# A fourth buffer for raw weights in the gate stage of a hybrid attention block, with evaluations one product later

## The chip, the cores and the metric

The kernel runs on one core of a Trainium2 chip. It is one launch: the weights and the input start in device memory (HBM) and the output ends there. The metric is the device time of the launch in microseconds (us). Five engines work beside each other, each in its own fixed order: PE (TensorE, matrix products), DVE (VectorE, elementwise), ACT (ScalarE, activation functions and copies), POOL (GpSimd) and SP (SyncE, which here only issues DMA transfers). They wait for each other through semaphores.

## The reference

Two layers of a transformer block on 512 tokens of width 1024, in float32. A layer is a feed-forward part, a token mix with three kinds of attention, and a second feed-forward part, with layer norms between. The change lies in the end of the token mix:

```python
o_a, o_b, o_c = _nsa(...), _swa_sink(...), _fox(...)            # each 512 x 512
g = jax.nn.sigmoid(h @ w_gate + b_gate).reshape(B, S, N_BRANCH, D)   # three gates, each 512 x 1024
merged = g[:, :, 0] * (o_a @ w_br_a) + g[:, :, 1] * (o_b @ w_br_b) + g[:, :, 2] * (o_c @ w_br_c)
return merged @ w_out
```

## The kernel before

All tiles have 128 partitions, and a float32 product is made of three products of a cheaper kind: each operand is split into a high part `hi` (a rounded copy, made by ACT) and a low part `lo` (what is left, by DVE), and PE computes hi·hi + hi·lo + lo·hi. So each block of weights goes through the same steps: SP issues the load of 512 KB into a buffer called `raw`; ACT writes `hi`; DVE writes `lo` and with that frees the `raw`; PE uses both. A branch's block is loaded by two transfers of 256 KB.

The `raw` buffers form a ring. In this stage it has three entries, all from the pool `wt`; `wraw()` takes the next one in turn, and the load into it waits on SP's queue until the DVE operation that read it last has ended. SP works through its loads strictly in order.

The gate stage computes for each of the three branches (`br` 0, 1, 2 for a, b, c) eight blocks `d` of 128 gate columns. The first few are computed by `plain` (24 products of 512 columns each, then a tanh on ACT, since the sigmoid is written by tanh). `branch` multiplies the attention output of a branch with two blocks of its weights, and DVE multiplies the result by the gate and adds it to `acc` (the `stt` and `tt` lines, called the evaluation here). From block (1, 6) on, `cycle` computes two gate blocks at a time by a Winograd scheme with 7 products for 8. An object `Two` holds the two raw blocks `rg` and `ru`; `sums` forms four sums of them on DVE (tile `ws`), and `hi("ug")`, `hi("u1")`, `hi("u2")`, `hi("ud")` split the four operands. A cycle's PE work is: `ga` (two products), `pa` (two), `pb` (one), two more into `ga`, then the branch products `brp` of the cycle. The two later products into `ga` overwrite what ACT copies out as `sn`, so PE waits there until that copy is done. Seven cycles follow each other: (1,6), (2,2), (2,4), (2,6), (0,2), (0,4), (0,6). The cycles (2,2) and (0,2) load two branch blocks, the others one; the second one's `hi` and `lo` go into the tile `wo`, and the attention output of the branch is split into `oh` and `ol` just before.

Through the whole stage PE, POOL, ACT and DVE run in the order in which the code is written (`in_order()`). SP's loads are ordered by the scheduler, from its own estimate of when a buffer comes free. `tick` lets POOL issue a transfer for a later stage (`ts`), paced by the tile named. PSUM tiles come from `ps()`, a ring of eight banks. The stage begins with `plain(2, 1)`, whose weights `gate_w(2, 1, wt)` are the first block loaded in it; before, that block is split while the last attention batch still runs. `gp` is the pool of this stage; its memory was the attention's before. `token_sums` makes the tile `mm` on which the Winograd products work, in steps (`some(2)`) between the first products.

Of the kernel before, what the change touches and what calls it, by code (L numbers as in the profile page):

```python
# [9 lines left out]
F32 = mybir.dt.float32  # L10
# [8 lines left out]
P = 128  # L19
S, D, F = 512, 1024, 2816  # L20
# [44 lines left out]
def body(tc, a, out, depth=DEPTH):  # L65
# [8 lines left out]
    wt = pool("wt")  # L74
# [6 lines left out]
    def ps(tag=None, name="ps", shape=(P, 512)):  # L81
        if tag is None:
            tag = PS_ALL[ring[0] % 8]
            ring[0] += 1
        return psp.tile(list(shape), F32, name=name, tag=tag, bufs=PS_TAGS[tag])
# [32 lines left out]
    def more_raws(p, n):  # L118
        raws.extendleft([(p, n)] * n)

    def less_raws(p):
        keep = [x for x in raws if x[0] is not p]
        raws.clear()
        raws.extend(keep)
# [6 lines left out]
    more = K()  # L131
# [44 lines left out]
    def mm3(o, w, k, vh, vl, first, last):  # L176
        hi, lo = w
        if lo is None:
            nc.tensor.matmul(o[0:64], hi[:, k, 0:64], vh, start=first, stop=False)
            nc.tensor.matmul(o[0:64], hi[:, k, 0:64], vl, start=False, stop=last)  # L180
            return
        nc.tensor.matmul(o, hi[:, k], vh, start=first, stop=False)  # L182
        nc.tensor.matmul(o, hi[:, k], vl, start=False, stop=False)  # L183
        nc.tensor.matmul(o, lo[:, k], vh, start=False, stop=last)  # L184
# [655 lines left out]
    def mix(l, wts, pend, done_ffn, xap, xa, nxt):  # L840
# [264 lines left out]
        class Swa:  # L1105
            br, nseg, ngrp = 1, 1, 1
# [53 lines left out]
        class Fox:  # L1160
            br, nseg, ngrp = 2, 2, 2
# [48 lines left out]
        class Nsa:  # L1210
            br, nseg = 0, 2
# [249 lines left out]
        def gate_ev(t, p, br, d):  # L1461
            nc.scalar.activation(t, p, AF.Tanh, scale=0.5, bias=bg[:, br, d:d + 1])
# [83 lines left out]
        gp = pool("gp", reuse_waits="tile")  # L1546
        acc = gp.tile([P, KD, S], F32, name="acc")
        ob = [gp.tile([P, 4, S], F32R, name=n) for n in ("oh", "ol")]
        gd = [gp.tile([P, 4, P], F32R, name=n) for n in ("dh", "dl")]
        g1 = [gp.tile([P, S], F32, name=f"g1{br}") for br in range(3)]  # L1550
        gw = a["w_gate"][l]
        tt, stt = nc.vector.tensor_tensor, nc.vector.scalar_tensor_tensor
        lo4, hi4, H1, H2 = slice(0, 4), slice(4, 8), slice(0, 256), slice(256, 512)
# [25 lines left out]
        def gate_w(br, d, pl):  # L1579
            r = raw_of(gw, br * D + d * P)  # L1580
            u = pair_of(pl)
            parts(*u, r)
            return u

        def branch_w(br, d, pl, now=True):
            r = wraw()
            v = wb[br].rearrange("(k p) f -> p k f", p=P)
            for j in range(2):
                nc.sync.dma_start(r[:, 4 * j:4 * j + 4], v[:, :, (d + j) * P:(d + j + 1) * P])
            if pl is op:  # L1590
                u = op.tile([P, 2, KD, P], F32R, name="wo", tag="o2")
                u = u[:, 0], u[:, 1]
            else:
                u = pair_of(pl)
            lo = high(*u, r)
            if not now:
                return u, lo
            lo()
            return u

        def tick(t):
            sums_step(t[:, 0:1] if len(t.shape) == 2 else t[:, 0, 0:1])
# [27 lines left out]
        class Two:  # L1630
# [14 lines left out]
            def hi(u, n):  # L1645
                x = {"ug": u.rg, "u1": u.x1, "u2": u.x2, "ud": u.ru[:, hi4]}[n] if n != "ug" else u.rg
                t = gd if n == "ud" else pair_of(more.pool if n == "ug" else wt)
                setattr(u, n, t)
                return high(*t, x)
# [11 lines left out]
        def gate_t(br, d):  # L1661
            g[br, d] = t = gp.tile([P, S], F32, name="t", tag="t", bufs=4)
            return t

        def plain(br, d, w, t=None):
            p = ps(name="gate")
            proj(p, w)
            t = gate_t(br, d) if t is None else t
            gate_ev(t, p, br, d)
            tick(t)  # L1670

        def branch(br, d, w, mid=None):
            for j in range(2):
                p = ps(name="brp")
                for k in range(4):
                    mm3(p, w, 4 * j + k, ob[0][:, k], ob[1][:, k], k == 0, k == 3)
                if mid and j == 0:
                    mid()
                t, o = g[br, d + j], acc[:, d + j]
                if br == 1:  # L1680
                    stt(o, t, 1.0, p, op0=OP.add, op1=OP.mult)
                else:
                    stt(t, t, 1.0, p, op0=OP.add, op1=OP.mult)
                    tt(o, o, t, op=OP.add)
            tick(o)

        def temp(n):
            return gp.tile([P, S], F32, name=n, tag=n, bufs=2)

        def cycle(cur, nxt, brps, end):  # L1690
            ga, pa, pb = (ps(name="gate") for _ in range(3))
            none = lambda: None
            hi = nxt.hi if nxt else lambda n: none
            if nxt:
                nxt.sums()
            ws = [branch_w(br, d, op if i else wt, False) for i, (br, d) in enumerate(brps)]
            lo = hi("ug")
            prod(ga[:, H1], cur.ug, 0, XP)
            prod(ga[:, H2], cur.u1, 0, T[0], False)
            sn, v, h = temp("sn"), temp("v"), gate_t(cur.br, cur.d + 1)  # L1700
            nc.scalar.activation(sn, ga, AF.Copy)
            for _, f in ws:
                f()
            lo()
            prod(pa[:, H1], cur.u1, 4, T[1])
            lo = hi("u1")
            prod(pa[:, H2], cur.u2, 0, T[2], False)
            tt(v[:, H1], pa[:, H1], sn[:, H1], op=OP.add)
            tt(v[:, H2], pa[:, H2], v[:, H1], op=OP.add)
            tt(h[:, H2], sn[:, H2], v[:, H2], op=OP.add)  # L1710
            lo()
            prod(pb[:, H1], cur.ud, 0, T[3])
            lo = hi("ud")
            tt(h[:, H1], pb[:, H1], v[:, H2], op=OP.add)
            prod(ga[:, H1], cur.ug, 4, XR, False)
            lo()
            nc.scalar.activation(h, h, AF.Tanh, scale=0.5, bias=bg[:, cur.br, cur.d + 1:cur.d + 2])
            prod(ga[:, H2], cur.u2, 4, XS, False)
            t = gate_t(cur.br, cur.d)
            lo = hi("u2") if nxt else end()  # L1720
            tt(ga[:, H2], ga[:, H2], v[:, H1], op=OP.add)
            gate_ev(t, ga, cur.br, cur.d)
            lo()
            tick(t)
            for (br, d), (w, _) in zip(brps, ws):
                branch(br, d, w)

        wp = [gate_w(2, 1, wt)]
        split_o(1)
# [4 lines left out]
        def some(n):  # L1734
            for _ in range(n):
                steps.pop(0)()

        plain(2, 1, wp[0], g1[2])
        wp.append(gate_w(1, 3, wt))
        some(2)  # L1740
        branch(1, 0, wp[1])
        wp.append(branch_w(1, 2, more.pool))
        plain(1, 2, wp[2])
        some(2)
        wp.append(gate_w(1, 4, wt))
        plain(1, 3, wp[3])
        some(2)
        wp.append(gate_w(1, 5, wt))
        branch(1, 2, wp[4])
        some(2)  # L1750
        wp.append(branch_w(1, 4, more.pool))
        cur = Two(1, 6)
        plain(1, 4, wp[5])
        some(2)
        plain(1, 5, wp[6])
        some(2)
        some(2)
        cur.sums()
        los = [cur.hi(n) for n in ("ug", "u1", "u2", "ud")]
        for f in los:  # L1760
            f()
        branch(1, 4, wp[7])
        todo = deque([(2, 2), (2, 4), (2, 6), (0, 2), (0, 4), (0, 6)])
        then = Two(*todo.popleft())
        brps = {(1, 6): [(1, 6)], (2, 2): [(2, 0), (2, 2)], (0, 2): [(0, 0), (0, 2)]}

        wo, ws_ = a["w_out"][l], []
# [1 line left out]
        def out_w(k):  # L1769
            r = wraw()  # L1770
            nc.sync.dma_start(r.rearrange("p k f -> p (k f)"), wo[k * P:(k + 1) * P, :])
            u = pair_of(wt if k else more.pool)
            ws_.append(u)
            return high(*u, r)
# [5 lines left out]
        while cur:  # L1780
            me = cur.br, cur.d
            if me[1] == 2:
                split_o(me[0])
            if not then:
                out_w(0)()
            cycle(cur, then, brps.get(me, [me]), merged)
            cur, then = then, Two(*todo.popleft()) if todo else None
        los = [out_w(k) for k in (1, 2)]
        for d in (6, 7):
            los.append(high(mh[:, d], ml[:, d], acc[:, d]))  # L1790
        for f in los:
            f()
        more.n = 3
        order.__exit__(None, None, None)
        gp.release()
# [22 lines left out]
    w = xl[:, KD - 1, 256:512].bitcast(BF)  # L1818
    nc.vector.memset(w, 1.0)
    o = ps("po", "warm")  # L1820
# [155 lines left out]
```

## Time and profile before

| What | us |
|---|---|
| Median of 3 runs (lowest, highest) | 2467.86 (2467.81, 2469.29) |
| Profiled execution: its own time | 2468.07 |
| Profiled execution: span from first to last instruction | 2466.4 |
| PE busy in the span | 2423.0 (98%) |
| DVE, ACT, POOL busy | 1949.1 (79%), 1228.2 (50%), 487.4 (20%) |
| Gate stage of the first layer, about | 666 to 840 |
| Gate stage of the second layer, about | 1892 to 2078 |

PE's share of the chain that ended last is 96%, so time is saved here where PE waits or runs slowly, and nowhere else. A row of the timeline gives the start, the duration, the engine and line, what is written and read, and in brackets how long the engine was idle before it and what released it. A row of windows gives the busy time of PE, PEld (weight loads of PE), DVE, ACT and POOL in a stretch, with their counts, then PEclk, the share of its full clock that TensorE was granted, then the DMA share and the rate.

### The profile page before, as it was taken

The page shows a single profiled execution, that of the slowest core. Times are in us where ns is not written, and L with a number is a line of the kernel's source. Part 1 is how long each engine was busy: PE and PEld are TensorE (multiplying, and loading weights), DVE is VectorE, ACT ScalarE, POOL GpSimd, SP SyncE. Part 2 cuts the span into 40 slices and gives each one's busy share as a digit, 9 for nine tenths or more (in the row PEclk, how much of TensorE's full clock was granted, in tenths as well). Part 3 has the DMA queues.
Part 4 walks back from the last instruction along what each step waited for, and adds up shares of the span by engine and source line. Part 5 has one row for each costly group of instructions (what it writes and reads, how often), then busy time and mean ns, then how long its engine had stood idle before and what let it go on. Part 6 is the DMA issues. An engine that isn't in the chain of part 4 may idle for free.

```text
span 2466.4 us, 41973 instructions
## 1 busy us (share of the span) xinstructions
PE 2423.0 (98%) x15952; PEld 2168.5 (88%) x15952; DVE 1949.1 (79%) x3782; ACT 1228.2 (50%) x2336; POOL 487.4 (20%) x684
## 2 busy tenths in 40 slices
PE   9999999999998999999999999999999889999998
PEld 8999887888888889998899998878888788899987
DVE  6899976677677659999879998666775776699997
ACT  4444645676633434445534456356775333344463
POOL 4232402244310001124000003022453000000040
PEclk9999999999999999999999999999999999999999
DMA  7888754676563536787533346456665535333373
GB/s 204 231 223 218 255 166 124 173 164 142 120 167 89 170 121 154 207 212 238 185 106 108 104 148 224 143 146 183 151 142 135 148 90 171 103 94 103 104 240 123
DMA packets 422586, 390.09 MB, mean 158 GB/s; under 512 B 20472, under 2 KB 352392, under 8 KB 422384
## 3 DMA queue, kind: packets, MB, share of 16 engines
q1 hardware_dynamic: 385792, 287.00, 39.1%
q0 software_dynamic: 36592, 100.41, 16.9%
q8 instruction: 126, 2.06, 0.3%
q14 instruction: 76, 0.62, 0.1%
HBM read 360.02 MB, written 93.38 MB: 184 GB/s over the span
## 4 chain that ended last, share of the span: by engine, by line
PE 96%; DVE 2%; DMA 1%; ACT 1%; issue 1%; POOL 0%; SPq 0%; DVEq 0%; POOLq 0%; ACTq 0%
PE acc L331 17%; PE pg L647 17%; PE pu L647 8%; PE pj L182 6%; PE pj L183 6%; PE pj L184 5%; PE gate L1656 5%; PE pv L647 4%; PE brp L184 2%; PE brp L182 2%; PE brp L183 2%; PE sN L1258 2%; PE ptN L1300 1%; PE po L1319 1%; PE acc L196 1%; PE acc L197 1%
## 5 line engine op out<-in xcount | busy, mean ns | idle before, releaser
L162 DVE TENSOR_TENSOR lo<-raw,hi 128x1024 fp32r<-128x1024 f32 (+2 forms) x186 | 217.2, 1186 | 88.9 <-ACT hi L161 87.9
L182 PE MATMUL pj<-xh,hi 128*128 128x512 f32 (+1 forms) x720 | 267.7, 372 | 0.6 <-ACT hi L161 0.6
L184 PE MATMUL pj<-xh,lo 128*128 128x512 f32 (+1 forms) x720 | 255.0, 354 | 0.4 <-DVE lo L162 0.4
L183 PE MATMUL pj<-xl,hi 128*128 128x512 f32 (+1 forms) x720 | 254.9, 354 | 0.0
L161 ACT ACTIVATE hi<-raw 128x1024 fp32r<-128x1024 f32 (+2 forms) x186 | 185.8, 1019 | 131.3 <-PE acc L331 52.9
L647 PE MATMUL pg<-xl,hi 128*128 128x256 f32 x864 | 244.5, 283 | 0.0
L647 PE MATMUL pg<-xh,lo 128*128 128x256 f32 x864 | 244.5, 283 | 0.0
L647 PE MATMUL pg<-xh,hi 128*128 128x256 f32 x864 | 244.5, 283 | 0.0
L331 PE MATMUL acc<-hi,sh 128*128 128x512 f32 x568 | 221.5, 390 | 0.0
L331 PE MATMUL acc<-lo,sh 128*128 128x512 f32 x568 | 221.0, 389 | 0.0
L331 PE MATMUL acc<-hi,sl 128*128 128x512 f32 x568 | 221.0, 389 | 0.0
L352 POOL COPY pace<-sh 64x1 f32<-64x1 f32 x16 | 94.6, 5915 | 474.6 <-ACT sh L592 474.6
L544 DVE TENSOR_TENSOR lo<-ws,hi 128x1024 fp32r<-128x1024 f32 x144 | 175.0, 1216 | 0.0
L647 PEld LDWEIGHTS pg<-xh,hi 128*128 128x128 f32 x864 | 165.9, 192 | 0.2
L647 PEld LDWEIGHTS pg<-xl,hi 128*128 128x128 f32 x864 | 165.9, 192 | 0.2
L647 PEld LDWEIGHTS pg<-xh,lo 128*128 128x128 f32 x864 | 165.9, 192 | 0.0
L647 PE MATMUL pu<-th,hi 128*128 128x256 f32 x576 | 163.0, 283 | 0.0
L647 PE MATMUL pu<-tl,hi 128*128 128x256 f32 x576 | 163.0, 283 | 0.0
L647 PE MATMUL pu<-th,lo 128*128 128x256 f32 x576 | 163.0, 283 | 0.0
L184 PEld LDWEIGHTS pj<-xh,lo 128*128 128x128 f32 x720 | 136.4, 189 | 20.3 <-DVE lo L162 0.6
L541 ACT ACTIVATE hi<-ws 128x1024 fp32r<-128x1024 f32 x144 | 144.1, 1048 | 16.9 <-DVE ws L526 15.3
L182 PEld LDWEIGHTS pj<-xh,hi 128*128 128x128 f32 x720 | 136.8, 190 | 16.4 <-issue 3.7
(418 smaller groups left out, 7094.3 us busy)
## 6 DMA issues: line engine op xcount, KB each, us to landing
raw<-in_ffn_w_dram SPq DMA_DIRECT2D x228, 512.0 KB, 4.5
ts<-in_ffn_w_dram POOLq DMA_DIRECT2D x72, 768.0 KB, 7.2
raw<-in_w_in_dram SPq DMA_DIRECT2D x56, 512.0 KB, 4.1
raw<-ts SPq DMA_DIRECT2D x52, 512.0 KB, 4.1
raw<-in_w_gate_dram SPq DMA_DIRECT2D x48, 512.0 KB, 4.1
ts<-ts POOLq DMA_DIRECT2D x24, 768.0 KB, 8.4
x_sp<-xa POOLq DMA_DIRECT2D x24, 512.0 KB, 6.2
ks<-hl SPq DMA_DIRECT2D x96, 128.0 KB, 2.6
```

What stands on the lines that cost most here:

```text
L161: nc.scalar.activation(hi[:, c], raw[:, c], AF.Copy)
L162: nc.vector.tensor_tensor(lo[:, c], raw[:, c], hi[:, c].bitcast(F32), op=OP.subtract)
L182: nc.tensor.matmul(o, hi[:, k], vh, start=first, stop=False)
L183: nc.tensor.matmul(o, hi[:, k], vl, start=False, stop=False)
L184: nc.tensor.matmul(o, lo[:, k], vh, start=False, stop=last)
L331: nc.tensor.matmul(o, xx[:, t], ww[:, c], start=first and i == 0, stop=last and i == 2)
L352: nc.gpsimd.tensor_copy(pace[0:64], sp(min(p + 1, NS - 1))[0][0:64, 0, 0:1].bitcast(F32))
L541: nc.scalar.activation(t[0], x, AF.Copy)
L544: nc.vector.tensor_tensor(t[1], x, t[0].bitcast(F32), op=OP.subtract)
L647: nc.tensor.matmul(o, wx, vx, start=first and k == 0 and i == 0, stop=k == 3 and i == 2, skip_group_check=True)
L1258: nc.tensor.matmul(o[:, 0:nb].rearrange("p k b j -> p (k b j)"), q, kx[:, 2 * b0:2 * (b0 + nb)].rearrange("p a b -> p (a b)"), start=i == ...
L1656: nc.tensor.matmul(o, wx, vx, start=first and k == 0 and i == 0, stop=k == 3 and i == 2, skip_group_check=True)
```

## The change

- The ring of `raw` buffers gets a fourth entry, in the pool `gp` (`more_raws(gp, 1)`), taken first; to make room `sn` and `v` have one buffer each instead of two.
- `plain` and `branch` return their evaluation instead of doing it; in the first part of the stage each is placed after the next product, so on ACT and DVE it comes behind the splits and sums for that next product.
- In `cycle` the raw blocks of the cycle after the next are requested before the branch products, the four sums of the next cycle stand on DVE before the evaluations of the branch products, and the last evaluation of a cycle goes into the next one, behind the copy `sn`.

PE and POOL keep their order. The core of the diff:

```diff
+        more_raws(gp, 1)
...
         def plain(br, d, w, t=None):
             p = ps(name="gate")
             proj(p, w)
-            t = gate_t(br, d) if t is None else t
-            gate_ev(t, p, br, d)
-            tick(t)
+            def ev():
+                o = gate_t(br, d) if t is None else t
+                gate_ev(o, p, br, d)
+                tick(o)
+            return [ev]
...
         def temp(n):
-            return gp.tile([P, S], F32, name=n, tag=n, bufs=2)
+            return gp.tile([P, S], F32, name=n, tag=n)
...
-        def cycle(cur, nxt, brps, end):
+        pend_ev = []
+        def cycle(cur, nxt, brps, load, end):
...
-            if nxt:
-                nxt.sums()
             ws = [branch_w(br, d, op if i else wt, False) for i, (br, d) in enumerate(brps)]
-            lo = hi("ug")
+            los = [f for _, f in ws] + [hi("ug")]
...
             nc.scalar.activation(sn, ga, AF.Copy)
-            for _, f in ws:
+            for f in pend_ev + los:
                 f()
-            lo()
+            pend_ev.clear()
...
-            for (br, d), (w, _) in zip(brps, ws):
-                branch(br, d, w)
+            new = load()
+            for i, ((br, d), (w, _)) in enumerate(zip(brps, ws)):
+                evs = [branch(br, d, w, j) for j in range(2)]
+                if new and not i:
+                    new.sums()
+                if i == len(brps) - 1:
+                    pend_ev.append(evs.pop())
+                for f in evs:
+                    f()
+            return new
...
-        plain(2, 1, wp[0], g1[2])
-        wp.append(gate_w(1, 3, wt))
         some(2)
-        branch(1, 0, wp[1])
...
+        evs = plain(2, 1, wp[0], g1[2])
+        for i, (go, prep) in enumerate((
+                (lambda: [branch(1, 0, wp[1], j) for j in range(2)], lambda: gate_w(1, 3, wt)),
+                (lambda: plain(1, 2, wp[2]), lambda: branch_w(1, 2, more.pool)),
...
+            w = prep()
+            some(2)
+            new = go()
+            for f in evs:
+                f()
+            evs = new
...
         los = [out_w(k) for k in (1, 2)]
+        pend_ev.pop()()
...
+        less_raws(gp)
```

Three places show what this does to the order. Numbers at the names tell tiles apart; a tile can have another number in the changed kernel. First, ACT at the start of the stage in the first layer, before (`raw_7773` is the block for `plain(2, 1)`, `raw_7783` the one for `branch(1, 0)`, `pj` are the last gate products of the attention stage):

```order
L1532 ACTIVATE o2_4103<-po_7721 128x128
L1532 ACTIVATE o0_4101<-po_7721 128x128
L1462 ACTIVATE g10_7766<-pj_7518,bgate_82 128x512
L1462 ACTIVATE g11_7767<-pj_7631,bgate_82 128x512
L1559 ACTIVATE oh_7762<-o1_4102 128x1024 x2
L1559 ACTIVATE hi_7786<-raw_7783 128x1024
```

And the same place after the change:

```order
L1532 ACTIVATE o2_4103<-po_7721 128x128
L1532 ACTIVATE o0_4101<-po_7721 128x128
L1462 ACTIVATE g10_7766<-pj_7518,bgate_82 128x512
L1462 ACTIVATE g11_7767<-pj_7631,bgate_82 128x512
L1560 ACTIVATE hi_7775<-raw_7773 128x1024
L1560 ACTIVATE oh_7762<-o1_4102 128x1024 x2
L1560 ACTIVATE hi_7786<-raw_7783 128x1024
```

The split of the first block, which stood earlier, among the work of the last attention batch, now stands behind the last attention output `o0`. Next, SP's loads around the cycles (1,6) and (2,2), before (`raw_8123` is the branch block of (1,6), `raw_8268` and `raw_8270` the gate blocks of (2,4), `raw_8284` and `raw_8290` the two branch blocks of (2,2)):

```order
L1589 DMA raw_8123<-in_w_br_b_dram 128x4x128 x2
L1576 DMA raw_8268<-in_w_gate_dram 128x8x128
L1576 DMA raw_8270<-in_w_gate_dram 128x8x128
L1589 DMA raw_8284<-in_w_br_c_dram 128x4x128 x2
L1589 DMA raw_8290<-in_w_br_c_dram 128x4x128 x2
L1576 DMA raw_8467<-in_w_gate_dram 128x8x128
```

And after (`raw_8121`, `raw_8240`, `raw_8242`, `raw_8283` and `raw_8289` are the same blocks; `raw_8407` belongs to (2,6)):

```order
L1590 DMA raw_8121<-in_w_br_b_dram 128x4x128 x2
L1577 DMA raw_8240<-in_w_gate_dram 128x8x128
L1590 DMA raw_8289<-in_w_br_c_dram 128x4x128 x2
L1577 DMA raw_8242<-in_w_gate_dram 128x8x128
L1590 DMA raw_8283<-in_w_br_c_dram 128x4x128 x2
L1577 DMA raw_8407<-in_w_gate_dram 128x8x128
```

Before, `raw_8290` reuses the buffer of `raw_8284`, the load just ahead of it. After, the second branch block stands first of the two; it takes the buffer of `raw_8121`, and `raw_8283` takes that of the block split as `dh` in the cycle (1,6). Last, DVE around the end of the cycle (2,2), before (`lo_8402` is the last split of that cycle, `brp_…` its branch products, `ws_8474` the sums for (2,6)):

```order
L1560 TENSOR_TENSOR lo_8402<-ws_8279,hi_8401 128x1024
L1683 SCALAR_TENSOR_TENSOR g02_4277<-g02_4277,brp_8407 128x512
L1684 TENSOR_TENSOR acc_7761<-acc_7761,g02_4277 128x512
...
L1684 TENSOR_TENSOR acc_7761<-acc_7761,t_8324 128x512
L1640 TENSOR_TENSOR ws_8474<-raw_8469 128x512
L1641 TENSOR_TENSOR ws_8474<-ws_8474,raw_8467 128x512
L1642 TENSOR_TENSOR ws_8474<-raw_8467,raw_8469 128x512
L1643 TENSOR_TENSOR ws_8474<-raw_8467,ws_8474 128x512
```

And after, where the same sums are `ws_8437`:

```order
L1561 TENSOR_TENSOR lo_8402<-ws_8270,hi_8401 128x1024
L1641 TENSOR_TENSOR ws_8437<-raw_8409 128x512
L1642 TENSOR_TENSOR ws_8437<-ws_8437,raw_8407 128x512
L1643 TENSOR_TENSOR ws_8437<-raw_8407,raw_8409 128x512
L1644 TENSOR_TENSOR ws_8437<-raw_8407,ws_8437 128x512
L1687 SCALAR_TENSOR_TENSOR g02_4277<-g02_4277,brp_8411 128x512
L1688 TENSOR_TENSOR acc_7761<-acc_7761,g02_4277 128x512
```

The four sums moved from behind the eight evaluation rows to ahead of them.

More of the change, by code (lines that the diff above doesn't have):

```diff
@@ L1667, in plain, with branch, ev @@
             proj(p, w)
-            t = gate_t(br, d) if t is None else t
-            gate_ev(t, p, br, d)
-            tick(t)
[L1672 to L1678, printed above, removed]
+            def ev():
[3 more added lines that the diff above has]
+            return [ev]
+        def branch(br, d, w, j):
+            p = ps(name="brp")
+            for k in range(4):
+                mm3(p, w, 4 * j + k, ob[0][:, k], ob[1][:, k], k == 0, k == 3)
+            def ev():
                 t, o = g[br, d + j], acc[:, d + j]
@@ L1684, in branch @@
                     tt(o, o, t, op=OP.add)
-            tick(o)
+                if j:
+                    tick(o)
+            return ev
         def temp(n):
-            return gp.tile([P, S], F32, name=n, tag=n, bufs=2)
-        def cycle(cur, nxt, brps, end):
+            return gp.tile([P, S], F32, name=n, tag=n)
+        pend_ev = []
+        def cycle(cur, nxt, brps, load, end):
             ga, pa, pb = (ps(name="gate") for _ in range(3))
@@ L1736, in some, with load @@
                 steps.pop(0)()
-        plain(2, 1, wp[0], g1[2])
-        wp.append(gate_w(1, 3, wt))
         some(2)
-        branch(1, 0, wp[1])
[L1742 to L1757, printed above, removed]
+        todo = deque([(1, 6), (2, 2), (2, 4), (2, 6), (0, 2), (0, 4), (0, 6)])
+        def load():
+            return Two(*todo.popleft()) if todo else None
+        evs = plain(2, 1, wp[0], g1[2])
+        for i, (go, prep) in enumerate((
+                (lambda: [branch(1, 0, wp[1], j) for j in range(2)], lambda: gate_w(1, 3, wt)),
+                (lambda: plain(1, 2, wp[2]), lambda: branch_w(1, 2, more.pool)),
+                (lambda: plain(1, 3, wp[3]), lambda: gate_w(1, 4, wt)),
+                (lambda: [branch(1, 2, wp[4], j) for j in range(2)], lambda: gate_w(1, 5, wt)),
+                (lambda: plain(1, 4, wp[5]), lambda: branch_w(1, 4, more.pool)),
+                (lambda: plain(1, 5, wp[6]), load))):
+            w = prep()
[4 more added lines that the diff above has]
+            evs = new
+            if i < 5:
+                wp.append(w)
+        cur = w
+        then = load()
         cur.sums()
         los = [cur.hi(n) for n in ("ug", "u1", "u2", "ud")]
-        for f in los:
-            f()
-        branch(1, 4, wp[7])
-        todo = deque([(2, 2), (2, 4), (2, 6), (0, 2), (0, 4), (0, 6)])
-        then = Two(*todo.popleft())
+        new = [branch(1, 4, wp[7], j) for j in range(2)]
+        for f in los + evs:
+            f()
+        then.sums()
+        pend_ev.extend(new)
         brps = {(1, 6): [(1, 6)], (2, 2): [(2, 0), (2, 2)], (0, 2): [(0, 0), (0, 2)]}
@@ L1785, in mix @@
                 out_w(0)()
-            cycle(cur, then, brps.get(me, [me]), merged)
-            cur, then = then, Two(*todo.popleft()) if todo else None
+            new = cycle(cur, then, brps.get(me, [me]), load, merged)
+            cur, then = then, new
         los = [out_w(k) for k in (1, 2)]
+        pend_ev.pop()()
         for d in (6, 7):
```

## The prediction

> **What bounds the kernel now.** I read the page first (engines, then the chain that ended last), then PE's waits, then the clock.
>
> ```profile
> PE 2423.0 (98%) x15952; PEld 2168.5 (88%) x15952; DVE 1949.1 (79%) x3782; ACT 1228.2 (50%) x2336; POOL 487.4 (20%) x684
> PE 96%; DVE 2%; DMA 1%; ACT 1%; issue 1%; POOL 0%; SPq 0%; DVEq 0%; POOLq 0%; ACTq 0%
> ```
>
> PE bounds the kernel. The change gives PE the same products in the same order, so it can only move PE's idle time and its clock. The waits of PE over the whole span begin with:
>
> ```profile
> PE gate L1656 <- ACT sn L1701: 25.1, 6, 6.6
> PE gate L1656 <- DVE lo L1560: 4.3, 2, 2.1
> PE hid L1030 <- DMA cw<-in_cmp_k_w_dram: 1.9, 2, 1.3
> ```
>
> Columns: total us, times, longest. Both lie in the cycles (L1656 is `prod`), and the third wait is already small, so nearly all of PE's waiting is in the stage that the change touches: 29.4 us, in four places per layer. The windows behind the three larger places of each layer show a second cost (the seventh number after the length and the comma is the granted clock, 0.66 in the first row):
>
> ```profile
> 713.10:718.10 5.00, 4.96 (x29) 4.96 (x30) 4.97 (x7) 0.53 (x2) 0.00 (x0) 0.66 0.53 157
> 743.80:748.80 5.00, 5.00 (x26) 4.96 (x27) 4.26 (x8) 2.35 (x4) 0.00 (x0) 0.61 0.72 210
> 804.60:809.60 5.00, 5.00 (x25) 5.00 (x26) 4.12 (x7) 2.10 (x3) 0.00 (x0) 0.54 0.72 207
> 1938.50:1943.50 5.00, 5.00 (x29) 5.00 (x30) 4.97 (x7) 0.46 (x1) 0.00 (x0) 0.66 0.55 164
> 1969.10:1974.10 5.00, 4.98 (x26) 4.94 (x27) 4.24 (x8) 2.34 (x4) 0.00 (x0) 0.60 0.68 201
> 2029.60:2034.60 5.00, 4.97 (x23) 4.97 (x24) 4.20 (x7) 2.17 (x3) 0.00 (x0) 0.51 0.72 204
> ```
>
> After each such stall PE works for about four us at half clock. Lost in each: 5 us times one minus the clock, 1.70, 1.95, 2.30, 1.70, 2.00 and 2.45, together 12.1 us. The stalls therefore cost 29.4 + 12.1 = 41.5 us, and that is the most that the change can give.
>
> **The change part by part.** *The fourth buffer and the earlier loads.* The two long stalls of a layer are in the cycles with two branch blocks. PE, ACT and the chain at the first of them:
>
> ```profile
> 743.78 0.58 PE L1656 MATMUL gate<-xh,hi 128*128 128x256 f32 x1 [5.78 <-ACT sn L1701]
> 741.24 1.06 ACT L1559 ACTIVATE wo<-raw 128x1024 fp32r<-128x1024 f32 x1 [8.38 <-DMA raw<-in_w_br_c_dram]
> 736.34 1.14 DVE lo L1560
> 737.50 0.37 SPq L1589
> 737.92 3.25 DMA raw<-in_w_br_c_dram
> 743.24 0.49 ACT sn L1701
> ```
>
> The load of the second branch block waits for the split of the first (DVE `lo`, ending 737.5), because it has that block's buffer; ACT stands at it, and `sn`, two rows behind on ACT, is what PE needs. After the change it takes the buffer of the branch block of (1,6), free some 15 us earlier, and the first branch block takes the one that `dl` frees. That row, the ACT row at which it is then needed, and the landing times in this stage (last number, median us):
>
> ```profile
> 725.83 0.68 DVE L1560 TENSOR_TENSOR dl<-raw,dh 128x512 fp32r<-128x512 f32 x1
> 731.81 1.05 ACT L1559 ACTIVATE hi<-raw 128x1024 fp32r<-128x1024 f32 x1
> raw<-in_w_gate_dram SPq DMA_DIRECT2D x16, 512.0 KB, 5.7
> raw<-in_w_br_a_dram SPq DMA_DIRECT2D x8, 256.0 KB, 4.4
> ```
>
> Issue at 726.5, the second half 0.5 later, 4.4 to land: 731.4, 0.4 before ACT wants it. ACT then does `hi`, `wo` and `hi` of the next gate block (at 1.05 each, 734.6 at most) and `sn` (0.49), done by about 735.1. The last product of `pb` starts at 737.72:
>
> ```profile
> 737.72 0.28 PE L1656 MATMUL gate<-mm,dl 128*128 128x256 f32 x1
> ```
>
> So PE does not wait, with 2.5 us in hand for a late load. The same holds at (0,2) with the loads of branch a. The small wait of (1,6) has ACT at a branch load, too, which now follows an earlier split:
>
> ```profile
> 722.21 0.38 PE L1656 MATMUL gate<-xh,hi 128*128 128x256 f32 x1 [0.37 <-ACT sn L1701]
> 719.67 2.01 ACT L1559 ACTIVATE hi<-raw 128x1024 fp32r<-128x1024 f32 x2 [6.04 <-DMA raw<-in_w_br_b_dram]
> ```
>
> I take all 25.1 us as gone. The transfers are the same in number and size.
>
> *Evaluations one product later.* The `lo` stall (2.14 us) ends the chain tanh, `mm`, `x`, sums, `lo`:
>
> ```profile
> 705.37 0.69 ACT L1462 ACTIVATE t<-gate,bgate 128x512 f32<-128x512 f32 x1 [4.23 <-PE gate L184]
> 713.14 0.38 PE L1656 MATMUL gate<-xh,lo 128*128 128x256 f32 x1 [2.14 <-DVE lo L1560]
> ```
>
> ACT waits 4.23 us for PE at a tanh that, after the change, comes behind the four splits of the first cycle. Everything behind it moves up by as much, more than the 2.14 needed: 4.3 us gone. The evaluations that wait instead have no reader before the next branch product or cycle, and PSUM has eight banks; for the two evaluations of a branch that means two banks held one product longer. Cost nothing, hidden by PE's own next product.
>
> *The first block of the stage.* It now goes into the buffer in `gp`, and its split stands behind the attention's last output. Rows of ACT and PE at that place, of the split before the change (ACT, DVE), and of DVE's last attention work:
>
> ```profile
> 667.03 1.27 ACT L1462 ACTIVATE g<-pj,bgate 128x512 f32<-128x512 f32 x2
> 668.17 2.03 ACT L1559 ACTIVATE oh<-o 128x1024 fp32r<-128x1024 f32 x2
> 665.94 0.72 PE L1319 MATMUL po<-p,v 128*64 128x128 f32 x10
> 667.15 0.40 PE L184 MATMUL gate<-xh,lo 128*128 128x512 f32 x1
> 643.52 1.05 ACT L1559 ACTIVATE hi<-raw 128x1024 fp32r<-128x1024 f32 x1
> 644.74 1.23 DVE L1560 TENSOR_TENSOR lo<-raw,hi 128x1024 fp32r<-128x1024 f32 x1
> 650.47 0.42 DVE L1098 CUSTOM_DVE_ANT_0 p<-sN,tab 128x256 f32<-128x256 f32 x1
> 661.23 0.69 DVE L885 COPY p<-ptN 128x512 f32<-128x512 f32 x1 [1.23 <-PE ptN L1300]
> ```
>
> ACT starts `hi` where `oh` started, 668.17, ends at 669.22; `lo` takes 1.23 more: 670.5. The third matmul of the stage, which ran at 667.15, needs that `lo`: PE loses 3.35 us per layer, 6.7 in all. This is a new stall, and it costs the clock too; the nearest row is the 2.14 us stall with 1.70, so 3.4 for two. The load waits for a DVE operation of the attention (in the built order the one of the 650.47 row); even behind DVE's last one, 661.92 + 5.7 = 667.6 is in time. Behind PE's last attention product, 666.66, it would be 672.4 and `lo` at 674.7: 7.5 us per layer. That is the upper end, 3.35 the value, zero the lower end, if ACT got to the split earlier.
>
> *The sums ahead of the evaluations* put 4 × 0.65 = 2.6 us of DVE work ahead of `ol` in the two cycles that split a new attention output, and `wo` must wait for `ol`. That eats up to 0.6 of the 2.5 us in hand; PE pays nothing. One buffer for `sn` and `v`: both are read within the cycle, no cost.
>
> *The attention's last batch.* ACT and DVE lose one split (1.05, 1.23) and a few rows there change places, one PSUM copy coming some 1.4 us later:
>
> ```profile
> 640.00:666.00 26.00, 26.00 (x208) 21.86 (x206) 13.81 (x48) 12.46 (x42) 12.36 (x21) 1.00 0.45 81
> ```
>
> PE is busy 26.00 of 26.00 us there and ACT under half, so I take zero; nothing can be gained, and 1.4 per layer may be lost.
>
> *Sum.* Gone: 29.4 + 12.1 = 41.5. New: 6.7 + 3.4 = 10.1. Net 31.4 us. The profiled execution took 2468.07, so 2436.7; the median of the runs is 0.2 lower, so **2436.5**.
>
> **The rivals.** *(A) The start stall costs no clock.* The gap is split in two (2.6 us, two matmuls, 0.8 us), and a clock that looks at longer stretches might not fall. Against it: the 2.14 us stall fell to 0.66 in both layers. Time 2436.5 − 3.4 = 2433.1. The Trainium skill says this in "TensorE: Matmul & The Clock Gate", Part 1: the clock halves after an idle window of about 3.4 us. By that rule the 2.14 us stall should have kept its clock; this trace disagrees.
>
> *(B) The first block lands late*, by the 7.5 us case above: 15.0 of stall, clock 2 × 2.45 = 4.9, so new costs of 19.9 for 10.1: 2446.3.
>
> *(C) Part of the double-branch stalls stays*, because branch loads land over 2.5 us later than the median, queued behind gate blocks. One us of stall in each of four places and 2.0 of clock: 12 more, 2448.5.
>
> *(D) No change that can be seen.* ACT is freed of the load and the same wait returns at `wo` behind `ol`, so that the two long stalls stay at three quarters: 0.75 × (24.4 + 8.7) = 24.8 given back (24.4 is 25.1 less the two small waits of (1,6), 8.7 the clock behind those four), 2461; with (B) besides, 2471. Little speaks for it, as `ol` ends 0.6 later where 2.5 are free.
>
> *(E) Slower: DVE stands at the sums.* They now wait for a gate block's load ahead of the evaluations and of the next cycle's `lo`. In the cycle (2,2) the load goes out when the `lo` in the first row below ends, and the sums come after the second:
>
> ```profile
> 743.47 1.22 DVE L1560 TENSOR_TENSOR lo<-raw,hi 128x1024 fp32r<-128x1024 f32 x1
> 749.66 1.23 DVE L1560 TENSOR_TENSOR lo<-ws,hi 128x1024 fp32r<-128x1024 f32 x1 [0.54 <-ACT hi L1559]
> PE brp L184: 33.6, 32
> ```
>
> That is 6.2 us against a landing of 5.7, hardly any reserve. But DVE can lose time: its idle time before the evaluations (the third row: total us, times) was 33.6 us for 14 cycles with their preludes, some 2.4 a cycle. With landings of x, PE would lose (x − 6.2 − 2.4) + 1.95 of clock in each of 12 cycles, and the gain of 31.4 is used up at x = 9.3 us. At 10.5 it is 12 × 3.85 = 46 us: 2483. Needed is a landing nearly twice the median.
>
> **How the numbers follow.** Forecast 0.63, A 0.12, B 0.08, C 0.10, D 0.03, E 0.04. The range of 8 in 10 or more runs from A with a little less stall at the start, 2431, to C, 2449; it takes in the 2.8 us of the attention and B. A change of 0.2% (5 us) is about what a measurement of this kernel can tell from none. Faster by more than that: the forecast, A, B, C, 0.93; within: 0.03; slower: 0.04.
>
> **What would show it.** In the profile after, `sn` and `lo` go from PE's waits in the cycles, and a new wait of PE at the first `gate` products (by `plain`, L182 and L184) of about 2.6 and 0.8 us per layer comes first in the list, with a granted clock near 0.66 in the five us behind it. ACT's waits for branch loads (8.4 us at `wo` in (2,2)) are gone. I am wrong if PE still waits for `sn` in (2,2) and (0,2), if the first wait is near 7 us, or if DVE idles over 2 us a cycle at the sums.

## The result and the profile after

| | before | after |
|---|---|---|
| Median of the runs, side by side (us) | 2468.57 (2467.81 to 2470.53) | 2433.74 (2432.91 to 2434.51) |
| Span of the profiled execution | 2466.4 | 2431.9 |
| PE busy | 2423.0 | 2412.5 |
| PE idle (span less busy) | 43.4 | 19.4 |
| Mean granted clock | 0.991 | 0.997 |

The change makes the kernel faster: after to before is 0.9858, with an interval of 0.9841 to 0.9875, or 34.8 us between the medians. The forecast was 2436.5, the range 2431 to 2449.

PE's busy time holds the same products in both kernels, so a difference in it is work at half clock, to within about a us: the four kernels below in which PE never works at half clock show 2407.9 to 2408.8. The 34.5 us between the two spans are 24.0 us of PE's idle time (43.4 − 19.4) and 10.5 us of busy time (2423.0 − 2412.5), most of it clock. PE's line of the page, then the head of the list of PE's waits (total us, times, longest):

```profile
PE 2412.5 (99%) x15952; PEld 2159.2 (89%) x15952; DVE 1947.7 (80%) x3782; ACT 1230.2 (51%) x2336; POOL 484.8 (20%) x684
...
PE gate L182 <- ACT hi L1560: 5.3, 2, 2.6
PE hid L1030 <- DMA cw<-in_cmp_k_w_dram: 2.1, 2, 1.6
...
PE gate L184 <- DVE lo L1561: 0.5, 1, 0.5
```

The 25.1 us for `sn` and the 4.3 us for `lo` in the cycles are gone, and a wait at the first products of the stage stands on top, once per layer. Its place in the first layer, from the timelines of PE, ACT and DVE (start, duration; in brackets the idle time and what ended it):

```profile
664.70 1.92 PE L1319 MATMUL po<-p,v 128*64 128x128 f32 x32
669.26 0.79 PE L182 MATMUL gate<-xh,hi 128*128 128x512 f32 x1 [2.64 <-ACT hi L1560]
...
670.52 0.80 PE L184 MATMUL gate<-xh,lo 128*128 128x512 f32 x1
...
667.00 1.27 ACT L1462 ACTIVATE g<-pj,bgate 128x512 f32<-128x512 f32 x2
668.14 1.07 ACT L1560 ACTIVATE hi<-raw 128x1024 fp32r<-128x1024 f32 x1
...
669.24 1.23 DVE L1561 TENSOR_TENSOR lo<-raw,hi 128x1024 fp32r<-128x1024 f32 x1 [7.36 <-ACT hi L1560]
```

ACT's `hi` has no bracket: the block was there, and the split had to wait for its turn behind the two tanh. PE's attention ends at 666.62 (666.66 before), so the attention's last batch lost nothing in the first layer. The half clock follows the wait; windows of 10 us from the start of the stage in the first layer, and from the end of the wait in the second (after the number of POOL's instructions comes the clock):

```profile
667.00:677.00 10.00, 7.70 (x19) 5.60 (x20) 7.76 (x7) 6.94 (x9) 0.00 (x0) 0.66 0.80 184
1876.70:1886.70 10.00, 9.41 (x34) 7.33 (x35) 9.87 (x10) 4.90 (x7) 0.00 (x0) 0.83 0.75 194
```

10 us times one minus the clock is 3.4 us in the first layer and 1.7 in the second, behind waits of the same 2.64 us. In the cycle (2,2), where PE stood for 5.78 us, the timelines of SP, ACT and PE now read:

```profile
718.37 0.93 SPq L1590 DMA_DIRECT2D raw<-in_w_br_c_dram  x2
...
725.78 0.92 SPq L1590 DMA_DIRECT2D raw<-in_w_br_c_dram  x2
...
734.34 1.06 ACT L1560 ACTIVATE wo<-raw 128x1024 fp32r<-128x1024 f32 x1 [0.34 <-DVE ol L1561]
...
736.26 0.58 ACT L1708 ACTIVATE sn<-gate 128x512 f32<-128x512 f32 x1
...
738.98 0.28 PE L1657 MATMUL gate<-xh,hi 128*128 128x256 f32 x1
```

Both branch blocks are requested 7 us or more before ACT wants them: the second one's at 718.37 for `wo` at 734.34, the first one's at 725.78 for a `hi` at 732.96. ACT waits 0.34 us for `ol` and not for a transfer (8.38 before); `sn` is done at 736.84, 2.1 us before PE needs it at 738.98.

### The profile page after: what moved, and what is told of

Same layout as the page of the kernel before. It is cut to its first block, busy times and chain, and to the rows that moved or that the text cites. A ratio compares the mean times of both kernels' runs of the same rounds, so it can differ in the third digit from the quotient of the medians.

```text
span 2431.9 us, 41993 instructions
## 1 busy us (share of the span) xinstructions
PE 2412.5 (99%) x15952; PEld 2159.2 (89%) x15952; DVE 1947.7 (80%) x3782; ACT 1230.2 (51%) x2336; POOL 484.8 (20%) x684
## 4 chain that ended last, share of the span: by engine, by line
PE 99%; DMA 0%; ACT 0%; issue 0%; DVE 0%; DVEq 0%; POOLq 0%; SPq 0%; POOL 0%; ACTq 0%
PE acc L331 18%; PE pg L647 17%; PE pu L647 9%; PE pj L182 6%; PE gate L1657 6%; PE pj L183 6%; PE pj L184 6%; PE pv L647 4%; PE brp L183 2%; PE brp L182 2%; PE brp L184 2%; PE sN L1258 2%; PE po L1319 1%; PE ptN L1300 1%; PE acc L196 1%; PE acc L197 1%
```

## Experiments

Times are medians; each group of kernels ran beside the kernel before, whose medians were 2468.9, 2469.6 and 2468.7. The lines of the changed kernel are quoted as its own.

| Kernel | Median | Span | PE busy | PE idle |
|---|---|---|---|---|
| before | 2468.6 | 2466.4 | 2423.0 | 43.4 |
| the change | 2433.7 | 2431.9 | 2412.5 | 19.4 |
| fourth buffer from the second block on | 2423.9 | 2422.6 | 2408.8 | 13.8 |
| first split ahead of the tanh | 2428.4 | 2425.9 | 2408.0 | 17.9 |
| the same, in two halves | 2426.0 | 2424.0 | 2407.9 | 16.1 |
| fourth buffer alone | 2440.8 | 2441.0 | 2417.5 | 23.5 |
| order alone | 2448.9 | 2447.7 | 2415.5 | 32.2 |
| first products as before | 2440.5 | 2438.6 | 2415.5 | 23.1 |
| sums at the cycle's start | 2433.5 | 2429.6 | 2408.9 | 20.7 |
| fourth buffer from the second block, sums at the cycle's start | 2424.4 | 2423.1 | 2408.3 | 14.8 |
| gate blocks in 8 transfers | 2434.6 | 2433.3 | 2413.0 | 20.3 |
| gate blocks in 16 transfers | 2567.7 | 2566.8 | 2441.7 | 125.1 |

### The start stall taken away

```diff
-        more_raws(gp, 1)
         gw = a["w_gate"][l]
...
         wp = [gate_w(2, 1, wt)]
+        more_raws(gp, 1)
```

> The changed kernel, with the fourth buffer joining the ring one block later: the stage's first gate block stays in a buffer of the weights' pool, as before the change, and its split stands among the last attention batch again; the first branch block takes the new buffer. Theory (the start stall is only the late split of the first block): PE's first matmuls of the stage start without a wait; between the last attention product and the first branch product the changed kernel took 11.55 and 10.28 us where 24 matmuls at 0.2275 take 5.46, so 6.1 + 4.8 = 10.9 us go: 2433.7 - 10.9 = 2422.8. Rival (the buffer in the attention's old memory is late whatever block it holds): the wait moves to the first branch product, 5.5 us later; its block still lands late, and at most half of the 10.9 comes back: 2428 or more. Rival (the extra split slows the attention's last batch): a PE wait appears before the stage and the time stays above 2427.

Measured: 2423.85 (2423.56 to 2424.33), ratio to before 0.9818, interval 0.9803 to 0.9832. PE's waits of this kernel hold nothing from the gate stage, and no clock is lost:

```profile
PE hid L1030 <- DMA cw<-in_cmp_k_w_dram: 1.7, 2, 1.3
PE warm L1843 <- DVE xl L1840: 1.5, 1, 1.5
PE pg L182 <- ACT ha L586: 1.1, 2, 0.6
...
core 0: 2422.6 us, clock 1.000
```

The 9.9 us, one less than expected, are 5.6 of idle time and 3.7 of busy time by the spans, and the rest is scatter of the runs. The new buffer is not late with the first branch block, and the extra split does not disturb the attention. This and the kernel with late sums further down are the fastest that ran, 0.6 us apart.

### A shorter start stall

```diff
-        for br in range(2):
-            gate_ev(g1[br], held[br], br, 1)
...
         wp = [gate_w(2, 1, wt)]
+        for br in range(2):
+            gate_ev(g1[br], held[br], br, 1)
```

> The changed kernel, with the split of the stage's first gate block on ACT ahead of the two tanh of the last attention gates (1.27 us for both) instead of behind them; everything else as in the change. PE's start wait of 2.64 us per layer becomes about 1.4, and the second wait, for the low part, stays. Theory 1 (every stall of over a us costs the same half clock): 2 x 1.2 less, 2433.7 - 2.4 = 2431.3. Theory 2 (the clock is set in pieces of fixed length, about 1.7 us lost for each that holds too much idle time; a shorter stall touches fewer of them): one or two pieces fewer as well, 2428 to 2430. Rival (the two tanh, now late, hold a bank that PE needs, or the branch work): 2434 or more.

Measured: 2428.40. The wait is 1.49 us and then 0.53, in both layers, and the clock stays at full speed behind both:

```profile
668.03 0.50 PE L182 MATMUL gate<-xh,hi 128*128 128x512 f32 x1 [1.49 <-ACT hi L1558]
...
666.00:676.00 10.00, 7.98 (x41) 6.15 (x38) 7.11 (x7) 7.28 (x10) 0.00 (x0) 1.00 0.79 161
1872.00:1882.00 10.00, 9.47 (x40) 7.52 (x41) 9.12 (x8) 5.83 (x7) 0.00 (x0) 1.00 0.79 195
```

So 5.3 us are won by moving a split ahead of 1.14 us of work on ACT (667.00 to 668.14 in the change): by the spans 1.5 of idle time and 4.5 of busy time. The clock gives back more than the wait itself, and the first theory falls. Splitting the block in halves as well:

```diff
-        wp = [gate_w(2, 1, wt)]
+        wp = [pair_of(wt)]
+        r0 = raw_of(gw, 2 * D + P)
+        los0 = [high(wp[0][0][:, c], wp[0][1][:, c], r0[:, c]) for c in (lo4, hi4)]
+        for f in los0:
+            f()
```

> As the kernel with the early split, and the split made in two halves (two instructions each on ACT and DVE), so that PE can start after half of it: waits of about 0.8 and 0.3 us per layer. Theory 2 (pieces of fixed length; waits this short leave the clock alone): the kernel without a start stall took 2423.9, plus 2 x 1.1 of waits: 2426. Theory 1 (any new stall costs 1.7 of clock or more): 2429.5 or more.

Measured: 2425.95. One wait of 1.06 us per layer is left, with the clock at 1.00 behind both. That is the second theory's number, though with one wait where it had two.

### Buffer and order apart

The kernel before with the buffer alone:

```diff
+        more_raws(gp, 1)
...
-            return gp.tile([P, S], F32, name=n, tag=n, bufs=2)
+            return gp.tile([P, S], F32, name=n, tag=n)
...
+        less_raws(gp)
```

> The kernel before with the fourth buffer alone, in the same place in the ring as in the change (and one buffer each for sn and v); no instruction of ACT or DVE is reordered by hand. Theory (the buffer carries the long stalls, the order carries the short one): the four long waits for sn and their half clock go (24.4 + 8.7), the two waits for lo in the first cycle stay (4.3 + 3.4 of clock), the start stall is there (10.9): the changed kernel's 2433.7 + 7.7 = 2441.4. Rival (the loads also need the new order, because the evaluations hold back the splits that free buffers): PE still waits 2 us or more for sn in the cycles (2,2) and (0,2), 2450 or more.

Measured: 2440.77. Its first two waits of PE:

```profile
PE gate L182 <- ACT hi L1560: 5.3, 2, 2.6
PE gate L1657 <- DVE lo L1561: 4.3, 2, 2.1
```

No wait for `sn` is left: the buffer alone removes all 25.1 us of them. From the first to the last branch product of a layer this kernel takes 161.76 us, the change 157.87. The wait of 2.14 us for `lo` and 1.7 of clock behind it are 3.84 of these 3.89 us, so with the buffer in place the earlier requests and the evaluation carried into the next cycle are worth nothing that can be seen. The reverse, the changed kernel without `more_raws` and `less_raws`:

> The changed kernel without the fourth buffer: three raw buffers, the new order of evaluations, sums and load requests. Theory: no start stall, no wait for lo; the second branch block again waits for the split of the first, so that PE waits about 5 us in each of the cycles (2,2) and (0,2) of both layers: of the 41.5 us of before, 4 x 5 of waits and about 8.5 of clock stay, 13 go: 2468.6 - 13 = 2455.6 (2451 to 2460). Rival (the earlier requests and the order are what removes the long stalls): near 2424, no PE wait over 1 us in the stage. Rival (with three buffers, DVE stands at the sums that are now ahead of the evaluations, since the next gate block comes late): waits in most cycles, 2468 or more.

Measured: 2448.93 (2446.27 to 2449.86), 2 us under the lower end of what was expected. The wait, and ACT in front of it:

```profile
PE gate L1656 <- ACT sn L1707: 18.0, 4, 4.7
...
735.53 1.06 ACT L1559 ACTIVATE wo<-raw 128x1024 fp32r<-128x1024 f32 x1 [6.88 <-DMA raw<-in_w_br_c_dram]
737.44 0.58 ACT L1707 ACTIVATE sn<-gate 128x512 f32<-128x512 f32 x1
```

The mechanism is the one of before: ACT at `wo`, waiting for the second branch block. The order alone still gives 20 us: it removes the wait for `lo` and the two small ones for `sn`, and shortens the four long ones from 24.4 us in all to 18.0. These are 4.5 us each rather than 5, and the clock behind them costs about 7 (PE busy 2415.5 against some 2408.5 in the kernels without it) rather than 8.5. The expectation also counted from 41.5 us of stalls in all, where the kernel without a start stall shows 45.0.

The start of the stage written as before, the rest as in the change:

```diff
-            new = go()
+        def now(evs):
             for f in evs:
                 f()
-            evs = new
...
+        now(plain(2, 1, wp[0], g1[2]))
+        wp.append(gate_w(1, 3, wt))
+        some(2)
+        br2(1, 0, wp[1])
...
```

(`now` evaluates at once, `br2` runs a branch's two products with an evaluation behind each.)

> The changed kernel, with the first products of the stage written as before: each evaluation directly behind its own product. Buffers, cycles, sums and loads are those of the change. Theory (the deferral at the start of the stage is what removed the wait for lo in the first cycle): a PE wait of about 2.1 us for lo comes back in both layers, with half clock behind it: 2433.7 + 4.3 + 3.4 = 2441.4. Rival (the earlier load or the sums ahead removed it): same as the changed kernel within 2 us.

Measured: 2440.51; the wait of 2.14 us for `lo` is back in both layers. So the order at the start of the stage, evaluations behind the splits and the steps of `mm` for the next product, is what removed it. The sums at the cycle's start:

```diff
             ga, pa, pb = (ps(name="gate") for _ in range(3))
+            if nxt:
+                nxt.sums()
...
-                if new and not i:
-                    new.sums()
...
-        then.sums()
         pend_ev.extend(new)
```

> The changed kernel, with the four sums of the next cycle at the start of that cycle on DVE, as before the change, instead of ahead of the evaluations of the branch products. Theory (the long stalls went with the buffer, the short one with the deferral at the stage's start; the place of the sums is worth nothing): 2433.7 within 2 us, no PE wait for sn or lo in the cycles. Rival (the sums must be early, or the splits that free the buffers come too late): PE waits for sn or lo again in the cycles, 2438 or more.

Measured: 2433.51, the time of the change, with the start stall as PE's only wait in the stage. Together with the fourth buffer from the second block on:

> The fourth buffer joining one block later (no start stall) and the sums at the start of the cycle as before the change, at once. If the sums' place is worth nothing and the start stall is a matter of its own, the time is that of the kernel without the start stall, 2423.9 within 1.5 us. If the early sums hid something behind the start stall: 2426 or more, with waits of PE in the cycles.

Measured: 2424.41 (2424.03 to 2424.76), within 0.6 us of the kernel without a start stall. The place of the sums is worth nothing that these runs can tell.

### Gate blocks that land later

```diff
-            nc.sync.dma_start(r[:, 0:n], w.rearrange("(k p) f -> p k f", p=P)[:, :, c0:c0 + P])
+            for k in range(n):
+                nc.sync.dma_start(r[:, k], w.rearrange("(k p) f -> p k f", p=P)[:, k, c0:c0 + P])
```

> The changed kernel, with each gate block of the stage loaded by eight transfers of 64 KB instead of one of 512 KB: SP needs about 8 x 0.46 = 3.7 us to issue a block, so its last part lands some 3.2 us later. It is the rival of the prediction in which DVE stands at the sums, in a mild form: in the cycle (2,2) of the changed kernel the later block was issued at 738.3 and the sums began at 744.3, 6.0 us for a landing of 4.1; 7.3 makes DVE wait 1.3 us there, and its idle time before the evaluations of that cycle (0.85 + 1.32) can hold that. By that reckoning PE loses nothing: 2433.7 within 3 us. If the reserve was overrated, PE waits about 1 us in each of 12 cycles with half clock behind many: 2450 or more. Rival (SP's queue, strictly in order, brings the branch blocks late): waits for sn in (2,2) and (0,2), 2440 or more.

Measured: 2434.58. SP issued sixteen transfers in 8.09 us, and DVE waited at the sums of (2,2):

```profile
735.55 8.09 SPq L1578 DMA_DIRECT2D raw<-in_w_gate_dram  x16
...
745.40 0.69 DVE L1642 TENSOR_TENSOR ws<-raw 128x512 f32<-128x512 f32 x1 [1.66 <-DMA raw<-in_w_gate_dram]
```

1.3 us was expected; PE has no new wait. At the sums of a later cycle (801.38) DVE waited 4.21 us for a gate block, also without a new wait of PE. So DVE has the reserve that was reckoned, and more in places; where it ends is not shown. Each transfer cut in two once more, by partitions (0 to 63 and 64 to 127):

> As the kernel with eight transfers a gate block, with sixteen of 32 KB: SP needs some 16 x 0.46 = 7.4 us to issue one block, so the first of two lands after about 4.1 + 6.9 = 11 us. The prediction's rival E put the point at which the gain is used up at a landing of 9.3 us; by its formula PE loses (11 - 8.6) + 1.95 = 4.4 us in each of 12 cycles: 2433.7 + 52 = 2486. If SP's queue is what counts (two blocks take 14.8 of the 15 to 16 us of a cycle, and the branch blocks stand behind them), the waits are for sn in ACT's order rather than for the sums, 2470 or more. If the reserve is far larger than reckoned: within 5 us of the change.

Measured: 2567.74, slower than before by 4%, where 2486 or so was expected, or 2470 and more if SP's queue is what counts. PE's first waits and SP's queue:

```profile
PE gate L1659 <- ACT sn L1710: 77.1, 12, 9.5
PE gate L1659 <- DVE lo L1561: 26.8, 2, 13.7
...
743.58 20.64 SPq L1579 DMA_DIRECT2D raw<-in_w_gate_dram  x32
764.32 2.18 SPq L1592 DMA_DIRECT2D raw<-in_w_br_c_dram  x4
```

An issue takes 0.65 us here (20.64 / 32), not 0.46, so two blocks need 20.6 us of SP, more than the 14.8 reckoned, and the branch blocks stand behind them. From 700 to 840 us SP waited for other engines and landings 11.4 us in all, so its queue is close to the bound. DVE stood at the sums as well, 79.4 us between 700 and 900, and this run does not tell the two apart. So the price per late us in the rival E is not tested by it; it shows only that late gate blocks can cost far more than the change gains, most of it in PE's waits for `sn`.

## Why the prediction was right, step by step

**The long waits.** Right, in mechanism and size: the wait for `sn` is gone in all six places, and the buffer alone does it. The 2.5 us in hand at (2,2) measured 2.1.

**The wait for `lo`.** Right: deferred evaluations remove it, 4.3 us of wait in two places, and writing the start as before brings it back.

**What all stalls cost together.** Right within 1.2 us for the cycles, too low for the whole kernel. The prediction said 29.4 + 12.1 = 41.5. By PE's timelines the stretch from the first to the last branch product took 179.30 and 179.18 us before and 157.87 in both layers after, 42.7 less. Between before and the kernel without a start stall lie 45.0 us by the medians, and in the spans 29.6 us of idle time and 14.2 of busy time (2423.0 − 2408.8). So the prediction's "the most that the change can give" was too low, and about 1.7 us of the rest lie outside the stage, behind a wait of 1.31 us for a transfer in the second layer's attention, in this execution of before and not in that of after:

```profile
1639.70:1649.70 10.00, 9.70 (x44) 7.49 (x45) 4.35 (x20) 2.65 (x11) 0.89 (x2) 0.83 0.57 170
```

No step of the change explains that part.

**The start stall.** Right in place and kind, and its 10.1 us measured 10.8: from the last attention product to the first branch product the change takes 11.55 and 10.28 us, before 5.53 and 5.54. Both terms were off, in opposite directions, so that the sum is in part luck. The first wait is 2.64 us as said (2.6). The second is 0.48 in the second layer where 0.75 was said and, in the first layer, too short for the list of waits, since the matmuls ahead of it ran at half clock and took up most of that time. Against 6.7 us of waits thus stand 5.8. Of the clock 3.4 was said and about 4.8 lost: PE worked 6.58 and 2.93 us at half clock, as the windows of exactly that clock show (the number after the comma is PE's busy time):

```profile
669.05:675.88 6.83, 6.58 (x15) 4.70 (x16) 6.64 (x6) 4.89 (x6) 0.00 (x0) 0.50 0.68 163
1877.37:1880.78 3.41, 2.93 (x7) 2.15 (x7) 3.41 (x4) 3.41 (x5) 0.00 (x0) 0.50 0.71 164
```

The difference of the busy times to the kernel without a start stall, 3.7 (2412.5 − 2408.8), is smaller, since that time varies by about a us at full clock too. Rival A had no clock loss here and rival B a late block; the trace shows neither. That the loss of clock is no fixed price was not in the prediction: it took the 1.70 of the 2.14 us wait for each layer, and the layers paid 3.3 and 1.5.

**Sums, attention, rivals.** The sums cost PE nothing and bring nothing; the attention lost nothing. C and D are refuted by the absence of any wait for `sn`. E asked for a landing of 9.3 us; in the first layer's stage the median is 4.1 here (5.7 before), in the second's 4.9 in both, and gate blocks in eight transfers, whose last part went out some 3.5 us later, cost PE nothing.

**The sum.** The spans differ by 34.5 us where 31.4 was said. The cycles gave 42.7 for 41.5 and the start took 10.8 for 10.1, so 32.0 is the change's own. Some 2.4 us more came between the two stages: from the last branch product of the first layer to the end of the second layer's attention before took 1040.52 us and after 1038.13, and 1.7 of that is the half clock in the attention of before. Most of what the forecast missed is thus no part of its mechanism.

## What to carry to other kernels

When two loads share a small ring, look which split frees the buffer that the second needs: if that split is itself the user of the first, one more buffer takes away the whole wait (25.1 us here). With that buffer in place the order of the evaluations gave 7 us more (2440.8 to 2433.7) and the place of the sums nothing. Where a new buffer joins a ring, let it take a block whose load and split can be late; here the first block of the stage was the wrong one, and one block later is worth 9.9 us more. A wait of PE has two prices, its length and the half clock behind it, and shortening it from 2.64 to 1.49 us took away all of the second in the execution profiled.

## What the runs showed of the hardware

The clock behind a wait of PE is lost in pieces and not in proportion. In windows of 10 us behind a wait the clock is 1.00, 0.83 or 0.66 to 0.67 for waits up to 2.64 us: nothing, 1.7 or 3.4 us lost.

| Wait of PE (us) | Times seen | Clock lost behind it (us) |
|---|---|---|
| 1.06 (start, in halves) | 2 | 0 |
| 1.1 to 1.7 (attention, second layer) | 11 | 0 ten times, 1.7 once |
| 1.49, then 0.53 | 2 | 0 |
| 2.14 | 6 | 1.7 five times, 0 once |
| 2.64, then up to 0.53 | 10 | 0 once, 1.7 four times, 3.4 five times |
| 4.3 to 4.7 | 4 | 1.7 three times, 2.3 once |
| 5.8 to 6.6 | 4 | 2.0 to 2.5 |

The table holds all kernels but the one with sixteen transfers.

The traces show the pieces. The clock in them is 1.00 or 0.50, and each stretch of half clock in which PE works lasts 3.41 us or a whole multiple of it. Within an execution these stretches start whole multiples of 3.413 us apart: in before at 713.59, 740.89, 802.33, 1642.01, 1938.97, 1966.28 and 2027.72, which is 8, 26, 272, 359, 367 and 385 such steps behind the first. So the clock is set anew at fixed times that the waits of the program do not move. In all but one case it goes by how long PE was idle between two of these times. Here are the windows from one such time to the next around the same wait of 2.14 us in the two layers of one execution (the kernel with the first products as before):

```profile
717.13:720.54 3.41, 1.48 (x12) 1.48 (x13) 3.41 (x5) 2.21 (x3) 0.00 (x0) 1.00 0.02 7
720.54:723.95 3.41, 3.41 (x18) 3.41 (x18) 3.38 (x6) 1.14 (x2) 0.00 (x0) 0.50 0.73 213
...
1925.45:1928.86 3.41, 1.50 (x8) 1.10 (x6) 3.38 (x5) 1.94 (x3) 0.00 (x0) 1.00 0.70 125
1928.86:1932.28 3.42, 3.19 (x26) 3.19 (x27) 3.42 (x5) 0.72 (x2) 0.00 (x0) 1.00 0.51 153
```

PE is idle for 1.93 us of the first window, and half clock follows; in the second layer the wait fell into two windows with 1.91 and 0.23 us, and none follows. Both lie close to the limit. In the kernels of the table, a full-clock window with 2.0 us or more of PE's idle time was followed by half clock in all 19 cases. One with less than 1.8 us was followed by full clock in every case but one (1.40 us, in the attention of before). Between 1.8 and 2.0 us both occur. Which part of a wait falls into one window is chance for the kernel: the 2.64 and 0.53 us of the second layer, with the sums at the cycle's start, fell into two windows as 1.67 and 1.51 us and cost no clock. Why one window of half clock follows in some cases and two in others, these runs do not show.

The longest waits do not lose most, since there the half clock begins before the wait ends. Behind the wait from 738.00 to 743.78 in before, PE works for only 3.94 of the 6.83 us at half clock:

```profile
740.89:747.72 6.83, 3.94 (x18) 3.94 (x19) 5.25 (x8) 4.09 (x6) 0.00 (x0) 0.50 0.41 120
```

The Trainium skill, "TensorE: Matmul & The Clock Gate", Part 1, says that the activity window is free-running, 4096 cycles or 3413 ns long, so that the cold stretch at a kernel's start varies from run to run. The trace agrees with that length: 3.41 us is the step measured here. The Trainium skill's condition there for the fall, an idle window of about 3.4 us, does not fit: 2.14 us of idle time sufficed five times in six, and one wait of 1.31 us did.

SP's issue of a transfer took 0.37 us for a gate block in one transfer (median), 0.43 for one of 64 KB (eight a block) and 0.60 for one of 32 KB over half the partitions (sixteen a block); with the gaps between them, a row of thirty-two took 0.65 each. The runs do not show whether the size, the partitions or the length of the row is the cause.
